# One 512-column product in place of two of 256, its streaming operand read in turns of 16 columns

## The chip, the cores and the metric

The kernel runs on one core of a Trainium2 chip. Its time is the device time of one execution in microseconds (us), as the median of several runs. TensorE multiplies 128x128 tiles of weights, which are loaded ahead of each product, with a streaming operand of up to 512 columns, and adds the results up in PSUM. VectorE, ScalarE and GpSimd do the elementwise work, and DMA queues bring the weights from HBM into SBUF.

## The reference

One layer of a hybrid encoder for 512 tokens of width 1024, in float32: two branches (a gated short convolution, and attention with a forget gate), their gated merge, a channel mixer with a hidden width of 2816, and three RMS norms.

```python
h = rms_norm(x, norm_mix_g[l])
proj = h @ w_in[l]
cb, cc, cin, q, k, v, f_logit, g_logit = jnp.split(proj, split_idx, axis=-1)
u = causal_dwconv(cc * cin, conv_mix_w[l])
y_conv = (cb * u) @ w_out_conv[l]
...
y_attn = o @ w_out_attn[l]
gates = jax.nn.sigmoid(g_logit + b_gate[l])
g_conv, g_attn = jnp.split(gates, 2, axis=-1)
x = x + (g_conv * y_conv + g_attn * y_attn) @ w_o[l]
h = rms_norm(x, norm_ffn_g[l])
up = causal_dwconv(h @ w_up[l], conv_ffn_w[l])
a, b = jnp.split(up, 2, axis=-1)
x = x + (jax.nn.silu(a) * b) @ w_down[l]
...
return rms_norm(x, norm_f_g)
```

## The kernel before

Activations lie transposed: 128 features on the partitions, the 512 tokens along the free dimension, one such block (`kb`) per 128 features. A product takes a 128x128 tile of weights as the stationary operand and streams tokens past it; a bank of PSUM holds 128 output features by 512 tokens, and the products over all input blocks add up in it.

Every float32 operand is split in two parts of the type float32r: a high part (a copy rounded by ScalarE, `wh`, `xgh`, `x1h`, `gh` ...) and a low part (the rest, by VectorE, `wl`, `xgl`, `x1l`, `gl` ...). `mm3` (line 166) multiplies three of the four combinations: high by high, low weights by high activations, high weights by low activations. It cuts the 512 tokens into two halves of 256 columns, so each call issues six products, each with its own load of weights: the two token halves with `wh` and `xh`, the two with `wl` and `xh`, the two with `wh` and `xl`. All products are kept in the order of the program.

Weights come in chunks of 128 rows by 1024 columns (512 KB) in one list, `stream`, whose order is that of use. `load` issues the DMAs three chunks ahead on the SyncE queue, `split` (line 138) makes the two parts one chunk ahead of TensorE (L151 on ScalarE, L152 on VectorE), into tiles `wh_...` and `wl_...` with two buffers each. The parts start at an offset within their tiles, `WOFF`: 0 elements for the high and 32 (128 bytes) for the low part. Pads (`PADL`, `PADR`) and this offset fix where operands lie. As the program is allocated, the activations that `mm3` streams start at a multiple of 512 bytes within a partition, the high weights 320 and the low weights 448 bytes past one; each tile of 128 columns is 512 bytes, so this holds for all of them.

The stages, with the names of their tiles: the v projection (`pa`, `pb`, L281 and L282, which stream the weights past the activations), q and k of the first two pairs of heads (`p_q`, `p_k`), attention (scores `s` at L410 and L411, transposes `tp` at L439, `attend` with `o` through `mm3` on 128 or 256 columns) with the remaining projections `p_in` put between its steps, then gates and the two branch outputs (`p_ga`, `p_gb`, `yc`, `ya`), the output projection `p_wo`, the mixer's up projection `p_up` (44 blocks of 128 features) and its down projection `pd` (8 blocks; the last is done in two token halves, `pdA` and `pdB`, so that the first half's norm and store can start early).

Of the kernel before, what the change touches and what calls it, by code (L numbers as in the profile page):

```python
# [9 lines left out]
F32R = mybir.dt.float32r  # L10
# [3 lines left out]
P = 128  # L14
# [12 lines left out]
NPP = 4  # L27
NCT = 5
BIG = 1e30
PADL, PADR = 48, 120  # L30


# [3 lines left out]
VW = 4 * HD + H  # L36
RC = 2 * (S + H)
WC = D + P
WOFF = {"h": 0, "l": 32}


@with_exitstack
def block_kernel(ctx, tc, xT, vecs, wv, win, wmix, wo, wup, wdn, outT):
# [3 lines left out]
    nc = tc.nc  # L47
# [3 lines left out]
    wp = ctx.enter_context(tc.tile_pool(name="wp", bufs=2))  # L51
    ps = ctx.enter_context(tc.tile_pool(name="ps", bufs=1, space=PSUM))

    def keep(ins):
        return tc.keep_in_program_order(ins)

    def bank(i, name):
        return ps.tile([P, S], F32, tag=f"b{i}", name=name)
# [14 lines left out]
    def col(i):  # L73
# [10 lines left out]
        out=strip[:, 3 * P :],  # L84
        in_=strip[:, 3 * P :],
        compare_op=ALU.is_ge,
        fill=BIG,
        base=0,
# [29 lines left out]
    for j in range(KB):  # L118
        for c in range(3):
            a, b = 8 * c * P, min(8 * c + 8, NP) * P  # L120
# [10 lines left out]
    def load(upto):  # L131
        for k in range(len(raws), min(upto, len(stream) - 1) + 1):
            nm, src, ncol = stream[k]
            raw = wp.tile([P, RC], F32, tag="raw", name=f"raw_{nm}", bufs=AHEAD + 1)[:, :ncol]
            keep((nc.scalar if k == 0 else nc.sync).dma_start(raw, src))
            raws.append(raw)

    def split(hl=None):

        k = len(parts)  # L140
        if k == len(stream):
            return
        nm, _, ncol = stream[k]
        load(k + AHEAD)
        hi, lo = hl or [
            wp.tile([P, WC], F32R, tag=f"w{x}", name=f"w{x}_{nm}", bufs=2)[:, WOFF[x] : WOFF[x] + ncol] for x in "hl"
        ]
        if k == 0:
            keep(nc.vector.tensor_copy(hi, raws[k]))
        else:  # L150
            order["hi"] = nc.scalar.activation(hi, raws[k], AF.Copy).ins  # L151
        order["lo"] = nc.vector.tensor_sub(lo, raws[k], hi.bitcast(F32)).ins  # L152
        parts.append((hi, lo))

    def chunk(name, hl=None):

        k = chunk.n
        chunk.n += 1
        assert stream[k][0] == name
        if len(parts) == k:  # L160
            split(hl)
        return parts[k]

    chunk.n = 0

    def mm3(out, wh, wl, xh, xl, start, stop):


        n = out.shape[-1]
        cut = [slice(a, a + 2 * P) for a in range(0, n, 2 * P)] if n > 2 * P else [slice(0, n)]  # L170
        trio = ((wh, xh), (wl, xh), (wh, xl))
        for i, (w, x) in enumerate(trio):
            for c, cs in enumerate(cut):
                keep(nc.tensor.matmul(  # L174
                    out[:, cs], w, x[:, cs],
                    start=start and i == 0 and c == 0,
                    stop=stop and i == 2 and c == len(cut) - 1,
                ))

    ex = cp.tile([P, NT], F32, tag="ex", name="ex")  # L180
    nc.gpsimd.memset(ex, -0.5)
# [44 lines left out]
    ap = at.enter_context(tc.tile_pool(name="ap", bufs=1, side="right"))  # L226
# [30 lines left out]
    for kb in range(KB):  # L257
        if kb + 2 < KB:
            load_x(kb + 2)
        wh, wl = chunk(f"v{kb}")  # L260
        x = xs[kb]
# [24 lines left out]
        trio = ((xgh, wh), (xgh, wl), (xgl, wh))  # L286
# [12 lines left out]
    def proj(idx, name, evac, bank):  # L299
        st = {}  # L300

        def half(i):
            if i == 0:
                st["w"] = chunk(f"in{idx}")
                st["p"] = bank(f"p_{name}")
            wh, wl = st["w"]
            for kb in range(4 * i, 4 * i + 4):
                ks = slice(kb * P, (kb + 1) * P)
                mm3(st["p"], wh[:, ks], wl[:, ks], xgh[:, kb, :], xgl[:, kb, :], kb == 0, kb == KB - 1)
            if i == 1:  # L310

                while len(parts) < chunk.n + 2:
                    split()
                with after_split():
                    evac(st["p"])

        return [lambda: half(0), lambda: half(1)]
# [127 lines left out]
    def attend(pr, half):  # L445
        o = bank(7, f"o{pr}{half}")
        nk = 2 * half + 2
        for e in range(2):
            th, tl = PT.pop((pr, e, half))
            for kb in range(nk):  # L450
                cs = slice(P, 2 * P) if kb == nk - 1 else slice(0, 2 * P)
                wh = vh[:, kb, pr, e : e + 2, :].rearrange("p a b -> p (a b)")
                wl = vl[:, kb, pr, e : e + 2, :].rearrange("p a b -> p (a b)")
                mm3(
                    o[:, cs], wh, wl, th[:, kb, cs], tl[:, kb, cs],
                    e == 0 and kb == 0, e == 1 and kb == nk - 1,
                )
        hs = slice(half * 2 * P, (half + 1) * 2 * P)
        nc.scalar.activation(oth[:, pr, hs], o[:, : 2 * P], AF.Copy)
        nc.vector.tensor_sub(otl[:, pr, hs], o[:, : 2 * P], oth.bitcast(F32)[:, pr, hs])  # L460


    def run_all(fs):
        for f in fs:
            f()

    split()
    split()

# [65 lines left out]
    for idx in late:  # L535
        kind, i = divmod(idx, 4)
# [7 lines left out]
    n = len(units)  # L544
    for i in range(n + LA):
        if i < n:
            scores(*units[i])
        take = 1 if i < n + LA - 1 else len(fill)
        for _ in range(min(take, len(fill))):
            fill.pop(0)()  # L550
        if 0 <= i - LT < n:
            transp(*units[i - LT])
        if 0 <= i - LA < n:
            pr, e, qb = units[i - LA]
            if e == 1 and qb % 2 == 1:
                attend(pr, qb // 2)
# [27 lines left out]
    for j in range(KB):  # L584
        gs = []
        if j == 0:
            evac_gate(0, gs)(gp[0])
            evac_gate(8, gs)(gp[1])
        else:
            run_all(proj(20 + j, f"ga{j}", evac_gate(j, gs), acc))  # L590
            run_all(proj(28 + j, f"gb{j}", evac_gate(8 + j, gs), acc))
        wh, wl = chunk(f"mix{j}")
        yc, ya = acc(f"yc{j}"), acc(f"ya{j}")
        for pp, hh, ll, o in ((yc, ych, ycl, 0), (ya, oth, otl, 4)):
            for k in range(4):
                ks = slice((o + k) * P, (o + k + 1) * P)
                mm3(pp, wh[:, ks], wl[:, ks], hh[:, k, :], ll[:, k, :], k == 0, k == 3)
        a, b = gs
        nc.vector.tensor_mul(a, a, yc)
        nc.vector.tensor_mul(b, b, ya)  # L600
        nc.gpsimd.tensor_add(a, a, b)
        nc.scalar.activation(mh[:, j, :], a, AF.Copy)
        nc.vector.tensor_sub(ml[:, j, :], a, mh.bitcast(F32)[:, j, :])
# [31 lines left out]
    def block(name, xh, xl):  # L635
        wh, wl = chunk(name)
        q = acc(f"p_{name}")
        for kb in range(KB):
            ks = slice(kb * P, (kb + 1) * P)
            mm3(q, wh[:, ks], wl[:, ks], xh[:, kb, :], xl[:, kb, :], kb == 0, kb == KB - 1)  # L640
        return q

    po = None
    for j in range(KB):
        if j == 0:
            po = lead(["wo0", "wo1"], mh, ml)
        p = po[j] if j < 2 else block(f"wo{j}", mh, ml)
# [13 lines left out]
    fp = ctx.enter_context(tc.tile_pool(name="fp", bufs=1))  # L661
# [6 lines left out]
    for j in range(NP):  # L668
# [12 lines left out]
        for s_ in range(2):  # L681
            p = pu[s_] if j == 0 else block(f"up{2 * j + s_}", x1h, x1l)
# [5 lines left out]
        a, b = uu  # L688
# [9 lines left out]
    def down(j, c, extra=False):  # L698
        k0 = 8 * c
        nk = min(8, NP - k0)  # L700
        hl = None
        if extra:
            hl = [
                fp.tile([P, WC], F32R, tag=f"wx{x}", name=f"wx{x}")[:, 80 + WOFF[x] :][:, : nk * P] for x in "hl"
            ]
        wh, wl = chunk(f"dn{j}{c}", hl)

        def f(p, ts, a=0, b=8):
            for k in range(a, min(b, nk)):
                ks = slice(k * P, (k + 1) * P)  # L710
                kb = k0 + k
                mm3(p, wh[:, ks], wl[:, ks], gh[:, kb, ts], gl[:, kb, ts], kb == 0, kb == NP - 1)

        return f

    full = slice(0, S)
    for j in range(KB - 1):
        p = bank(j % 4, f"pd{j}")
        for c in range(3):
            down(j, c)(p, full)  # L720
        nc.vector.tensor_add(x1[:, j, :], p, x1[:, j, :])
        square_into(ssq3, x1[:, j, :], j == 0, fp, f"sq3_{j}")
        nc.scalar.activation(x1[:, j, :], x1[:, j, :], AF.Copy, scale=col(GF + j))
# [16 lines left out]
    def fin_out(i, rc):  # L740
        hs = halves[i]
        pb = rstd_bc(rc, 2, i, f"n3{i}")[:, : S // 2]
        for g, (a, b) in enumerate(((0, 1), (1, 3), (3, 5), (5, 7), (7, 8))):
            y = x1[:, a:b, hs]
            nc.vector.tensor_mul(y, y, pb.unsqueeze(1).to_broadcast([P, b - a, S // 2]))
            keep((nc.sync, nc.scalar)[g % 2].dma_start(outT[:, a:b, hs], y))

    d0, d1, d2 = down(j, 0, True), down(j, 1), down(j, 2)
    for d in (d0, d1, d2):
        d(ph[0], halves[0])  # L750
# [91 lines left out]
```

## Time and profile before

| | us |
|---|---|
| median of 3 runs | 731.8 (730.42 to 734.79) |
| the profiled execution: its time | 734.09 |
| the profiled execution: its span, first to last instruction | 732.3 |
| VectorE busy in it | 400.5 |
| ScalarE busy in it | 292.7 |
| GpSimd busy in it | 140.6 |

The profile counts TensorE's products as PE and its loads of weights as PEld. Products are pipelined: the recorded time of one (the "mean ns") reaches from its start to its last result and overlaps the next, so the pace has to be read from the distance of starts, or from a stretch of time and the count of products in it. In a group's row, 128*128 is the size of the weights and 128x256 the streaming operand's partitions by columns.

### The profile page before, as it was taken

The numbers are of one execution on the slowest core, as the hardware profiler recorded it, in microseconds if no ns is written. First come the engines' busy times: TensorE is split into PE (matmuls) and PEld (weight loads), VectorE is DVE, ScalarE is ACT, GpSimd is POOL, SyncE is SP. The second block draws the span as 40 slices with busy tenths as digits, with TensorE's granted clock in tenths as the row PEclk, the third lists the DMA queues.
The fourth block names the chain that finished last, engine by engine and source line by source line (L and its number), as shares of the span: only waits on it lengthen the run. The fifth ranks groups of instructions, "written<-read, shape, count | busy, mean of one in ns | idle before, by whom it ended". The sixth has DMA issues, their size and how long they took to land.

```text
span 732.3 us, 14449 instructions
## 1 busy us (share of the span) xinstructions
PE 717.3 (98%) x6220; PEld 715.0 (98%) x6220; DVE 400.5 (55%) x582; ACT 292.7 (40%) x447; POOL 140.6 (19%) x158
## 2 busy tenths in 40 slices
PE   8989999999999999999999999999999999999995
PEld 7889999999999999999999999999999999999995
DVE  6477666765445445454456666666666673223323
ACT  6374545544433332333344344343353442222321
POOL 6515434322001000113311011101101100000100
PEclk9999999999999999999999999999999999999998
DMA  6523222221222332533313332332322423333303
GB/s 211 162 68 104 77 83 60 59 86 58 88 87 87 90 112 88 166 112 129 114 59 116 94 108 87 106 98 87 115 88 87 115 80 102 88 100 100 110 1 115
DMA packets 23296, 71.39 MB, mean 97 GB/s; under 512 B 2976, under 2 KB 5408, under 8 KB 23232
## 3 DMA queue, kind: packets, MB, share of 16 engines
q1 hardware_dynamic: 20848, 66.98, 29.7%
q0 software_dynamic: 1152, 2.17, 1.0%
q10 hardware_dynamic: 1232, 1.32, 0.6%
q8 instruction: 49, 0.80, 0.5%
q14 instruction: 15, 0.12, 0.1%
HBM read 68.29 MB, written 2.10 MB: 96 GB/s over the span
## 4 chain that ended last, share of the span: by engine, by line
PE 92%; DVE 2%; DMA 2%; ACT 1%; issue 1%; SPq 0%; POOLq 0%; POOL 0%; DVEq 0%; ACTq 0%
PE p_up L174 33%; PE pd L174 14%; PE p_in L174 14%; PE p_wo L174 6%; PE p_gb L174 5%; PE p_ga L174 5%; PE yc L174 3%; PE ya L174 3%; PE o L174 2%; DMA xs<-in_xT_dram 2%; PE tp L439 1%; PE pdA L174 1%; PE p_k L174 1%; PE s L410 1%; PE s L411 1%
## 5 line engine op out<-in xcount | busy, mean ns | idle before, releaser
L174 PE MATMUL p_up<-x1h,wh_up 128*128 128x256 f32 x704 | 137.3, 276 | 0.0
L174 PE MATMUL p_up<-x1l,wh_up 128*128 128x256 f32 x704 | 137.1, 276 | 0.0
L174 PE MATMUL p_up<-x1h,wl_up 128*128 128x256 f32 x704 | 137.0, 276 | 0.0
L174 PEld LDWEIGHTS p_up<-x1h,wh_up 128*128 128x128 f32 x704 | 106.1, 188 | 0.0
L174 PEld LDWEIGHTS p_up<-x1l,wh_up 128*128 128x128 f32 x704 | 106.0, 188 | 0.0
L174 PEld LDWEIGHTS p_up<-x1h,wl_up 128*128 128x128 f32 x704 | 105.9, 188 | 0.0
L690 POOL TENSOR_TENSOR fu<-fu,fu 128x512 f32<-128x512 f32 x22 | 28.4, 1293 | 211.2 <-DVE fu L368 198.3
L152 DVE TENSOR_TENSOR wl_in<-raw_in,wh_in 128x1024 fp32r<-128x1024 f32 x36 | 50.3, 1398 | 30.9 <-ACT wh_in L151 30.4
L152 DVE TENSOR_TENSOR wl_up<-raw_up,wh_up 128x1024 fp32r<-128x1024 f32 x44 | 53.7, 1220 | 14.5 <-ACT wh_up L151 14.5
L174 PE MATMUL pd<-gl,wh_dn 128*128 128x256 f32 x308 | 60.1, 276 | 0.0
L174 PE MATMUL pd<-gh,wh_dn 128*128 128x256 f32 x308 | 59.9, 276 | 0.0
L174 PE MATMUL pd<-gh,wl_dn 128*128 128x256 f32 x308 | 59.9, 276 | 0.0
L174 PE MATMUL p_in<-xgh,wh_in 128*128 128x256 f32 x288 | 56.8, 279 | 0.0
L174 PE MATMUL p_in<-xgl,wh_in 128*128 128x256 f32 x288 | 56.4, 277 | 0.0
L174 PE MATMUL p_in<-xgh,wl_in 128*128 128x256 f32 x288 | 56.4, 277 | 0.0
L152 DVE TENSOR_TENSOR wl_dn<-raw_dn,wh_dn 128x1024 fp32r<-128x1024 f32 (+1 forms) x23 | 26.0, 1132 | 54.9 <-ACT wh_dn L151 54.8
L151 ACT ACTIVATE wh_up<-raw_up 128x1024 fp32r<-128x1024 f32 x44 | 46.4, 1055 | 22.3 <-issue 13.4
L151 ACT ACTIVATE wh_in<-raw_in 128x1024 fp32r<-128x1024 f32 x36 | 38.2, 1061 | 42.5 <-PE ya L174 12.7
L151 ACT ACTIVATE wh_dn<-raw_dn 128x1024 fp32r<-128x1024 f32 (+1 forms) x23 | 22.7, 985 | 66.5 <-PE pd L174 66.2
L174 PEld LDWEIGHTS pd<-gl,wh_dn 128*128 128x128 f32 x308 | 46.5, 188 | 0.0
L174 PEld LDWEIGHTS pd<-gh,wh_dn 128*128 128x128 f32 x308 | 46.3, 188 | 0.0
L174 PEld LDWEIGHTS pd<-gh,wl_dn 128*128 128x128 f32 x308 | 46.3, 188 | 0.0
(223 smaller groups left out, 1611.7 us busy)
## 6 DMA issues: line engine op xcount, KB each, us to landing
raw_up<-in_wup_dram SPq DMA_DIRECT2D x44, 512.0 KB, 3.5
raw_in<-in_win_dram SPq DMA_DIRECT2D x36, 512.0 KB, 3.5
raw_dn<-in_wdn_dram SPq DMA_DIRECT2D x16, 512.0 KB, 3.5
raw_mix<-in_wmix_dram SPq DMA_DIRECT2D x8, 512.0 KB, 3.6
raw_wo<-in_wo_dram SPq DMA_DIRECT2D x8, 512.0 KB, 3.9
raw_dn<-in_wdn_dram SPq DMA_DIRECT2D x8, 384.0 KB, 3.3
xr<-in_xT_dram POOLq DMA_DIRECT2D x8, 256.0 KB, 3.8
raw_v<-in_wv_dram SPq DMA_DIRECT2D x7, 260.0 KB, 4.9
```

The source lines that it names most:

```text
L151: order["hi"] = nc.scalar.activation(hi, raws[k], AF.Copy).ins
L152: order["lo"] = nc.vector.tensor_sub(lo, raws[k], hi.bitcast(F32)).ins
L174: keep(nc.tensor.matmul(out[:, cs], w, x[:, cs], start=start and i == 0 and c == 0, stop=stop and i == 2 and c == len(cut) - 1,))
L410: keep(nc.tensor.matmul(s[:, :nn], QT[pr][:, e, qs], KA[pr][:, e, :nn], start=True, stop=False))
L411: keep(nc.tensor.matmul(s[:, :nn], QB[pr % 2][: KR[e], e, qs], KBt[pr % 2][: KR[e], e, :nn], start=False, stop=True))
L439: keep(nc.tensor.transpose(tp[:, ks], pt[:, ks], ident))
L690: nc.gpsimd.tensor_mul(a, a, b)
```

## The change

`mm3` issues three products of 512 columns where it issued six of 256. The streaming operand and the output are read and written through a pattern of three steps: with `h=2`, `c=16`, the 512 columns count as two halves of 16 groups of 16 columns, and the groups of the two halves follow each other in turn (columns 0 to 15, 256 to 271, 16 to 31, 272 to 287 ...). The output is written in the same turns, so each result lands where it did. `attend`, whose operands have 128 or 256 columns, passes `plain=True` and reads in order. The last down block, which calls `mm3` with 256 columns, takes turns between two runs of 128.

Both parts of the weights start 16 elements (64 bytes) into their tiles. As the program is allocated, every weight tile that `mm3` uses then lies 384 bytes past its streaming operand, modulo 512.

```diff
+GC = 16
...
-WOFF = {"h": 0, "l": 32}
+WOFF = 16
...
-            wp.tile([P, WC], F32R, tag=f"w{x}", name=f"w{x}_{nm}", bufs=2)[:, WOFF[x] : WOFF[x] + ncol] for x in "hl"
+            wp.tile([P, WC], F32R, tag=f"w{x}", name=f"w{x}_{nm}", bufs=2)[:, WOFF : WOFF + ncol] for x in "hl"
...
-    def mm3(out, wh, wl, xh, xl, start, stop):
-
-
-        n = out.shape[-1]
-        cut = [slice(a, a + 2 * P) for a in range(0, n, 2 * P)] if n > 2 * P else [slice(0, n)]
-        trio = ((wh, xh), (wl, xh), (wh, xl))
-        for i, (w, x) in enumerate(trio):
-            for c, cs in enumerate(cut):
-                keep(nc.tensor.matmul(
-                    out[:, cs], w, x[:, cs],
-                    start=start and i == 0 and c == 0,
-                    stop=stop and i == 2 and c == len(cut) - 1,
-                ))
+    def turns(ap):
+
+        return ap.rearrange("p (h i c) -> p i h c", h=2, c=GC)
+
+    def mm3(out, wh, wl, xh, xl, start, stop, plain=False):
+
+        f = (lambda ap: ap) if plain else turns
+        keep(nc.tensor.matmul(f(out), wh, f(xh), start=start, stop=False))
+        keep(nc.tensor.matmul(f(out), wl, f(xh), start=False, stop=False))
+        keep(nc.tensor.matmul(f(out), wh, f(xl), start=False, stop=stop))
...
-                    e == 0 and kb == 0, e == 1 and kb == nk - 1,
+                    e == 0 and kb == 0, e == 1 and kb == nk - 1, plain=True,
...
-                fp.tile([P, WC], F32R, tag=f"wx{x}", name=f"wx{x}")[:, 80 + WOFF[x] :][:, : nk * P] for x in "hl"
+                fp.tile([P, WC], F32R, tag=f"wx{x}", name=f"wx{x}")[:, 80 + WOFF :][:, : nk * P] for x in "hl"
```

## The prediction

> **What bounds the kernel now.** I read the page first (share of each engine, chain of waits), then a table of the engines' busy time by stage, then the groups of TensorE products by shape, then single instructions in the timeline.
>
> ```profile
> span 732.3 us, 14449 instructions
> PE 717.3 (98%) x6220; PEld 715.0 (98%) x6220; DVE 400.5 (55%) x582; ACT 292.7 (40%) x447; POOL 140.6 (19%) x158
> PE 92%; DVE 2%; DMA 2%; ACT 1%; issue 1%; SPq 0%; POOLq 0%; POOL 0%; DVEq 0%; ACTq 0%
> ```
>
> TensorE is the path: 92% of the chain. PE has exactly as many weight loads (PEld) as products, and both are busy 98%, so it is still open which of the two sets the pace. The stages (start and end, then busy time and instructions of each engine, granted clock, DMA):
>
> ```profile
> core 0: us, PE busy (x) PEld busy (x) DVE busy (x) ACT busy (x) POOL busy (x), PEclk, DMA share, GB/s
> 0.00:62.00 62.00, 54.75 (x417) 53.50 (x418) 40.20 (x60) 34.77 (x61) 30.46 (x46) 0.94 0.47 143
> 62.00:194.00 132.00, 132.00 (x1130) 131.32 (x1129) 85.20 (x193) 62.33 (x139) 41.66 (x59) 1.00 0.24 75
> 194.00:360.00 166.00, 166.00 (x1466) 166.00 (x1465) 78.45 (x85) 58.02 (x70) 25.54 (x22) 1.00 0.35 108
> 360.00:602.00 242.00, 242.00 (x2137) 242.00 (x2136) 156.97 (x198) 103.46 (x135) 30.00 (x23) 1.00 0.32 96
> 602.00:706.00 104.00, 104.00 (x920) 104.00 (x920) 31.74 (x32) 30.14 (x36) 10.07 (x6) 1.00 0.30 89
> ```
>
> From 194 to 706 us one product starts every 113 ns (242.00 us / 2137 = 113.2; 166.00 / 1466 = 113.2; 104.00 / 920 = 113.0). What sets 113 ns? An attention product of 128 columns stands beside others of 256:
>
> ```profile
> 122.57 0.22 PE L174 MATMUL o<-pth,vh 128*128 128x128 f32 x1
> 122.63 0.28 PE L174 MATMUL o<-pth,vl 128*128 128x128 f32 x1
> 122.74 0.27 PE L174 MATMUL o<-ptl,vh 128*128 128x128 f32 x1
> 122.85 0.33 PE L174 MATMUL o<-pth,vh 128*128 128x256 f32 x1
> ```
>
> The first occupies TensorE for 0.06 us (122.57 to 122.63), but the next two, with as few columns, take 0.11 us each: the time of a 256-column product. Half the columns and the same pitch means that the load of the next weights is what is waited for, one per 0.11 us. So the paired 256-column products of today run at the pace of their loads, and each weight tile is loaded twice, once for each token half.
>
> **The change: what it removes.** `mm3` issues one 512-column product for each pair, so half the loads go. The pairs follow from the loops, and these groups confirm them (each tile has three such rows):
>
> ```profile
> L174 PE MATMUL p_up<-x1h,wh_up 128*128 128x256 f32 x704 | 137.3, 276 | 0.0
> L174 PE MATMUL pd<-gh,wh_dn 128*128 128x256 f32 x308 | 59.9, 276 | 0.0
> L174 PE MATMUL p_in<-xgh,wh_in 128*128 128x256 f32 x288 | 56.8, 279 | 0.0
> L174 PE MATMUL p_wo<-mh,wh_wo 128*128 128x256 f32 x128 | 25.0, 276 | 0.0
> L174 PE MATMUL p_ga<-xgh,wh_in 128*128 128x256 f32 x112 | 21.8, 276 | 0.0
> L174 PE MATMUL yc<-ych,wh_mix 128*128 128x256 f32 x64 | 12.5, 277 | 0.0
> ```
>
> Pairs: p_up 704 x 3 / 2 = 1056, pd 462, p_wo 192, p_ga and p_gb 168 each, yc and ya 96 each: 2238 steady pairs at 2 x 113.25 = 226.5 ns. p_in has 432 pairs that run a little slower, since scores and transposes break the rhythm:
>
> ```profile
> 96.50 2.76 PE p_in L174 x24
> ```
>
> 2.76 us / 12 pairs = 230 ns. p_q and p_k (48 pairs each) lie before 62 us, in the stage that waits for splits and in part runs at half clock.
>
> **What it adds: a 512-column product, whose load is hidden.** With 0.11 us per load and over 0.21 us per product the load no longer sets the pace; the columns do. The trace has plain 512-column products only among the scores:
>
> ```profile
> 177.47 0.39 PE L411 MATMUL s<-kb,qb 128*128 128x512 f32 x1
> 177.47 0.42 PEld L174 LDWEIGHTS p_in<-xgh,wh_in 128*128 128x128 f32 x2
> 177.70 0.40 PE L174 MATMUL p_in<-xgh,wh_in 128*128 128x256 f32 x2
> ```
>
> and, as groups by shape (us busy, mean ns of one):
>
> ```profile
> L174 PE MATMUL o<-pth,vh 128*128 128x128 f32 x16 | 3.5, 220 | 0.0
> L411 PE MATMUL s<-kb,qb 128*128 128x512 f32 x4 | 1.6, 392 | 0.0
> L411 PE MATMUL s<-kb,qb 68*128 68x512 f32 x4 | 1.6, 397 | 0.0
> L411 PE MATMUL s<-kb,qb 128*128 128x384 f32 x4 | 1.3, 337 | 0.0
> ```
>
> Upper end: the L411 product has its weights in place and still holds TensorE from 177.47 to 177.70, 230 ns, more than a pair of today's (226.5). Its recorded 392 ns thus holds some 162 ns that overlap the next product; the other L411 form, 397, gives 235. The next load starts in the same instant (177.47), so it reads SBUF while the product streams.
>
> Lower end: the rate of the columns alone. At half clock the columns, not the loads, set the pace:
>
> ```profile
> 56.13 0.63 PE L174 MATMUL p_k<-xgl,wh_in 128*128 128x256 f32 x2
> 56.55 0.63 PE L174 MATMUL p_k<-xgh,wh_in 128*128 128x256 f32 x2
> 56.98 0.63 PE L174 MATMUL p_k<-xgh,wl_in 128*128 128x256 f32 x2
> ```
>
> ```profile
> 56.00:57.00 1.00, 1.00 (x7) 1.00 (x7) 0.30 (x2) 0.86 (x2) 0.84 (x3) 0.50 0.81 70
> ```
>
> Four products take 0.85 us (56.13 to 56.98) at clock 0.50: 0.83 ns a column, 0.415 at full clock, so 512 columns need 213 ns and no layout gets below that.
>
> Value taken: the 128-column product that did not wait is the cleanest row: 220 ns recorded, less 162 to 163 of overlap, 57 to 58 ns, which is also its 0.06 us in the timeline. With 384 more columns at 0.415 (159 ns) this is **217 ns**. It assumes that a product's extra over its columns is paid once (4 ns), so that the further 13 ns of L411 are stalls between its reading and the load's, and that the change removes them. The reason to believe this lies in the addresses, not in a row: turned, the product walks 512 bytes (modulo 512) in 256 columns, some 107 ns, and a load reads its 512 bytes in about the same time. Both run at one pace, 384 bytes apart, where plain reading would overtake the load once. That fails if the load reads from the other end; no row shows its direction.
>
> The Trainium skill disagrees on the cause: its page "TensorE: Matmul & The Clock Gate", section "Step-by-step: what each phase is for", says that weights have a read port of their own and take nothing from the streaming operand, and "Back-to-back issue gap" gives N / 2.4 + 2.5 ns, an estimate of 215.8 ns for 512 columns in any layout. The 230 ns above are against it for plain reading; by it, the gain would be an estimated 30 us and the turns would be idle.
>
> **Moved and left alone.** The offset of the split weights (320 and 448 bytes before, 384 for both now, modulo 512) also moves the stream of the v products (L281, L282, 384 of them). These range from 118 to 122 ns now; going to 113 or rising as much is 384 x 7 ns = under 3 us in a stage that partly waits for splits: taken as 0. The last output block (132 half-width products) stays at the pace of its loads; at most its 15 jumps of address each show, 15 x 0.415 x 132 = 0.8 us; taken as 0. Attention's `attend` keeps plain reading. A few split and evacuation steps on VectorE and ScalarE change order within attention; these engines have slack there (85 and 62 of 132 us). DMA, splits and evacuations keep their counts, and what covers them shrinks to 24 x 217 = 5.2 us per chunk:
>
> ```profile
> L152 DVE TENSOR_TENSOR wl_up<-raw_up,wh_up 128x1024 fp32r<-128x1024 f32 x44 | 53.7, 1220 | 14.5 <-ACT wh_up L151 14.5
> L151 ACT ACTIVATE wh_up<-raw_up 128x1024 fp32r<-128x1024 f32 x44 | 46.4, 1055 | 22.3 <-issue 13.4
> raw_up<-in_wup_dram SPq DMA_DIRECT2D x44, 512.0 KB, 3.5
> ```
>
> 1.06 us + 1.22 us of split and a landing of 3.5 us, asked for three chunks ahead, still fit. VectorE, next in line, goes from 157 of 242 us to 157 of 231 in p_up. If the split became late, TensorE would wait at a chunk's start; nothing near that shows.
>
> **The sum.** Steady: 2238 x (226.5 - 217) = 21.3 us. p_in: 432 x (230 - 217) = 5.6 us. p_q and p_k: 0.3 us (the few that wait for nothing). Together 27.2 us, so a span of 705.1 from 732.3. The profiled execution took 734.1, 2.3 above the median of the runs (731.8); against that median, **705 us** (731.8 - 27.2 = 704.6). Of its own unknowns: 213 ns gives 731.8 - 37.6 = 694, 220 ns 714.
>
> **The rivals.**
> Columns that cost more (C). From L411, 384 to 512 columns, 392 - 337 = 55 ns per 128, not 53. Then 57 + 3 x 55 = 222 ns, saving 2238 x 4.5 + 432 x 8 = 13.5 us: 718 us. For it: the two shapes follow each other in the same code. Against: a conflict with the load is in both, and it is what the change aims at.
>
> The turns do not avoid the stall (B), the change not doing what it says: the price is that of L411, 230 to 235 ns. 2238 x 3.5 = 7.8 us more (p_in unchanged), 740 us; at 235 ns 2238 x 8.5 + 432 x 5 = 21 us, 753. For it: weights read from the other end would still cross the stream.
>
> The jumps cost (A), the other side. Each product leaps 31 times between halves, in what it reads and in what it writes to PSUM; no product of this profile has a broken pattern, so a jump's price is bounded below by 0 and above, as an estimate, by two column times of the half-clock row. It decides from (226.5 - 217) / 31 = 0.31 ns, three quarters of a column. At one column (0.415 ns) a product is 230 ns and the time 739; at two, 243 ns, 2238 x 16.5 + 432 x 13 = 42.5 us more: 774. Against it: each run is 16 columns long, 64 bytes. The Trainium skill speaks for it: "PSUM — Partial Sum Buffer", section "Specifications (TRN2)", says that any non-contiguous pattern slows matmuls significantly. No run here shows it yet.
>
> The gain is lost to another engine or eaten half by A or B (225 to 229 ns): 728 to 736.
>
> **How the numbers follow.** Forecast (214 to 220 ns, 697 to 714 us) 0.62; C 0.13; A 0.13; B 0.07; the last, about no change, 0.05. Half a percent (3.7 us) is what a measurement of this kernel can tell. Faster 0.62 + 0.13 = 0.75, same 0.05, slower 0.13 + 0.07 = 0.20. The range goes from 696 (1 us for the v products) over C and the case of no change to the mild ends of A and B, 740; the likeliest case alone is 697 to 714.
>
> **What would show it.** Right: PE and PEld near 3450 instructions; p_up groups of x352 with 128x512; starts 217 ns apart; PE still over 97% busy but PEld far below, since loads fall to about half the time; p_up's stage 230 to 232 us instead of 242. A or B: same counts, starts 230 ns or more apart (B near L411's 230 to 235, A anywhere above, and alike in all stages). C: 222 ns. Another engine: idle PE before chunks, released by DVE wl or ACT wh. I am wrong if the pitch is 226 or more, or if the pitch falls and the span does not.

## The result, and the profile after

The changed kernel takes 767.88 us (median of 4 runs, 767.46 to 768.49), beside 732.64 us for the kernel before in the same measurement: a ratio of 1.0482, 95% interval 1.0447 to 1.0516. It is 4.8% slower, where 705 us and 3.7% faster were forecast, and outside the range of 696 to 740.

From the page of the profile after, the span, the engines' shares, the chain by engine, and the group of one p_up product:

```profile
span 765.8 us, 8917 instructions
PE 751.9 (98%) x3454; PEld 609.3 (80%) x3454; DVE 400.9 (52%) x582; ACT 293.4 (38%) x447; POOL 140.5 (18%) x158
PE 93%; DMA 2%; DVE 2%; ACT 1%; issue 1%; POOL 0%; SPq 0%; POOLq 0%; DVEq 0%; ACTq 0%
L174 PE MATMUL p_up<-x1h,wh_up 128*128 128x512 f32 x352 | 142.0, 403 | 0.0
```

The change did what it says: 6220 - 2766 = 3454 products and as many loads, and the loads now rest a fifth of the time (80% busy). TensorE is still 93% of the chain and never waits in p_up (idle 0.0). So nothing else became the bound: each product of 512 columns itself takes longer. The timeline shows by how much:

```profile
420.20 0.40 PE L175 MATMUL p_up<-x1h,wl_up 128*128 128x512 f32 x1
420.44 0.40 PE L176 MATMUL p_up<-x1l,wh_up 128*128 128x512 f32 x1
420.68 0.40 PE L174 MATMUL p_up<-x1h,wh_up 128*128 128x512 f32 x1
```

One start every 0.24 us: 240 ns, where a pair took 226.5 and the forecast had 217. The recorded 403 ns less 240 leave 163 ns of overlap with the next product, the amount that the prediction found (162 to 163), so at full clock, and where nothing is waited for, recorded times can again be turned into distances of starts. The stages after (start and end, busy time and instructions of each engine, clock, DMA), cut where p_in, the gates, p_up and pd begin and end:

```profile
0.00:61.00 61.00, 54.94 (x327) 48.12 (x328) 39.85 (x59) 34.47 (x61) 29.96 (x46) 1.00 0.44 145
61.00:197.00 136.00, 136.00 (x694) 112.63 (x693) 85.70 (x194) 63.67 (x140) 42.22 (x59) 1.00 0.22 73
197.00:373.00 176.00, 176.00 (x747) 139.91 (x746) 78.51 (x85) 57.92 (x70) 25.53 (x22) 1.00 0.31 102
373.00:628.00 255.00, 255.00 (x1072) 202.24 (x1072) 156.96 (x197) 103.06 (x134) 29.87 (x23) 1.00 0.28 91
628.00:739.00 111.00, 111.00 (x464) 87.86 (x463) 31.94 (x32) 30.31 (x36) 10.12 (x6) 1.00 0.28 82
```

Every stage that `mm3` fills grew alike: p_up from 242 to 255 us, pd from 104 to 111, the gates and output projections from 166 to 176. By the prediction's own sum, 2238 x (240 - 226.5) = 30.2 us and 432 x some 10.5 = 4.5 us for p_in, together 34.7; the span grew by 33.5. The first stage gave about 1.7 us back: p_in begins at 61 instead of 62.6 us, and the stage ran at clock 1.00 instead of 0.94.

### The profile page after: what moved, and what is told of

Its sections match the earlier page's. It is cut to its first block, busy times and chain, and to the rows that moved or that the text cites. A ratio compares the mean times of both kernels' runs of the same rounds, so it can differ in the third digit from the quotient of the medians.

```text
span 765.8 us, 8917 instructions
## 1 busy us (share of the span) xinstructions
PE 751.9 (98%) x3454; PEld 609.3 (80%) x3454; DVE 400.9 (52%) x582; ACT 293.4 (38%) x447; POOL 140.5 (18%) x158
## 4 chain that ended last, share of the span: by engine, by line
PE 93%; DMA 2%; DVE 2%; ACT 1%; issue 1%; POOL 0%; SPq 0%; POOLq 0%; DVEq 0%; ACTq 0%
PE p_up L174 11%; PE p_up L176 11%; PE p_up L175 11%; PE pd L176 5%; PE pd L175 5%; PE pd L174 5%; PE p_in L174 5%; PE p_in L176 5%; PE p_in L175 5%; PE p_wo L176 2%; PE p_wo L175 2%; PE p_wo L174 2%; PE p_gb L176 2%; PE p_gb L175 2%; PE p_gb L174 2%; PE p_ga L176 2%
## 5 line engine op out<-in xcount | busy, mean ns | idle before, releaser
L174 PE MATMUL p_up<-x1h,wh_up 128*128 128x512 f32 x352 | 142.0, 403 | 0.0
L175 PE MATMUL p_up<-x1h,wl_up 128*128 128x512 f32 x352 | 141.9, 403 | 0.0
L176 PE MATMUL p_up<-x1l,wh_up 128*128 128x512 f32 x352 | 141.9, 403 | 0.0
L174 PEld LDWEIGHTS p_up<-x1h,wh_up 128*128 128x128 f32 x352 | 66.9, 190 | 17.5
L174 PE MATMUL pd<-gh,wh_dn 128*128 128x512 f32 x154 | 62.1, 403 | 0.0
L175 PE MATMUL pd<-gh,wl_dn 128*128 128x512 f32 x154 | 62.1, 403 | 0.0
L176 PE MATMUL pd<-gl,wh_dn 128*128 128x512 f32 x154 | 62.1, 403 | 0.0
L174 PE MATMUL p_in<-xgh,wh_in 128*128 128x512 f32 x144 | 58.3, 405 | 0.0
L176 PE MATMUL p_in<-xgl,wh_in 128*128 128x512 f32 x144 | 58.0, 403 | 0.0
L175 PE MATMUL p_in<-xgh,wl_in 128*128 128x512 f32 x144 | 58.0, 403 | 0.0
L682 DVE TENSOR_TENSOR fz<-p_up,rb_n 128x512 f32<-128x512 f32 x44 | 30.2, 688 | 35.0 <-PE p_up L176 34.8
```

Source lines behind the costliest of these rows:

```text
L174: keep(nc.tensor.matmul(f(out), wh, f(xh), start=start, stop=False))
L175: keep(nc.tensor.matmul(f(out), wl, f(xh), start=False, stop=False))
L176: keep(nc.tensor.matmul(f(out), wh, f(xl), start=False, stop=stop))
L682: nc.vector.tensor_mul(z, p, rb2)
```

## The experiments

What had to be told apart: whether the leaps of the address cost the time (theory J), the streaming operand meeting the load of the next weights in SBUF (theory S), or the columns themselves (theories C and F); whether reading or writing pays; and what part the offset of the weights has. (These letters, and the B and P that join them below, name theories of the experiments, not the rivals of the prediction.) Several experiments make the blocks of p_up in different ways within one kernel, so that their distances of starts can be read from one profile; their names end in letters that stand for the offset or the size.

**Turns taken out.** The 512-column products are read and written in order, with everything else as after the change.

```diff
-        f = (lambda ap: ap) if plain else turns
+        f = lambda ap: ap
```

> The change without the turns: 512-column products read and written in order, weights 384 bytes past. Theory J (each leap between halves costs one column time, 0.415 ns, 31 per product; the profile after shows 240 ns per product): 240 - 13 = 227 ns per product, so 2670 x 13 = 35 us less than after, about 733, equal to before. Theory S (the stalls come from the weight load meeting the stream, and turning makes that worse or better): plain reading overtakes the load once, as in L411, 230 ns or more, 740 us or above. Theory C (a column costs more than 0.415 ns whatever the order): 240 ns as after, 768 us.

Measured: 747.64 us (before in the same measurement 733.16; ratio 1.0209, 1.0164 to 1.0255). The turns cost 767.9 - 747.6 = 20.2 us; the other 14.5 us of the loss are there without them. The group of p_up in this kernel:

```profile
L175 PE MATMUL p_up<-x1h,wl_up 128*128 128x512 f32 x352 | 138.9, 395 | 0.0
```

395 - 163 = 232 ns, between what J (227) and the change (240) would have. J has the direction, but the size is the one that S gave (230 ns or more, 740 us or above).

**The offset alone.** The kernel before, 256-column products, with the weights' offset of the change.

```diff
-WOFF = {"h": 0, "l": 32}
+WOFF = {"h": 16, "l": 16}
```

> The kernel before with only the offset of the weights changed: both parts 384 bytes past, products still 256 columns each. If the pace of 113 ns is that of the weight load alone (my prediction) or the offset does not matter: 113 ns and 732 us. If the offsets of 320 and 448 avoid stalls that 384 brings (theory S): 116 to 120 ns a product as pdA and pdB show after the change (120), up to 5532 x 6.7 = 37 us more, 769.

Measured: 760.52 us (ratio 1.038, 1.0339 to 1.0422), nearly as slow as the change.

```profile
L174 PE MATMUL p_up<-x1h,wl_up 128*128 128x256 f32 x704 | 140.9, 281 | 0.0
```

281 instead of 276 ns each, 5 x 5532 = 28 us. The stream and the load of the weights do get in each other's way: 64 bytes of offset are worth 27 us, and a pace set by the loads alone, whatever the stream does, would not have moved.

**Offsets by order of reading.** In the blocks of p_up:

```diff
+        how, c, m = mode or (("p" if plain else "t"), GC, P)
+        rd = turned(c) if how in "tr" else same
+        wr = turned(c) if how in "tw" else same
...
+        v = PLAN.get(int(nm[2:])) if nm[:2] == "up" else None
+        wo_ = 16 * v[2] if v else WOFF
```

> The change with the blocks of p_up made in 24 ways, one after the other: plain 512, turned 512, and split 256, each at eight offsets of the weights (a to h: 320, 384, 448, 0, 64, 128, 192, 256 bytes past the stream modulo 512). Read is the distance of starts in each. Theory J: turned 240 ns and plain 227 at every offset, split 113 everywhere. Theory S: each of the three moves by 5 to 15 ns with the offset, and turned at some offset falls to 217 to 227.

The chain of waits of this kernel gives the time of each block's 24 products (48 when split); its columns are start, length, what:

```profile
386.51 5.59 PE p_plain_a L187 x24
403.18 5.45 PE p_plain_d L187 x24
430.77 5.76 PE p_turn_a L187 x24
448.05 5.76 PE p_turn_d L187 x24
476.85 5.46 PE p_split_a L187 x48
488.00 5.65 PE p_split_c L187 x48
493.65 5.75 PE p_split_d L187 x48
```

Divide by 24. Read in order, a product takes 227 ns at offsets of 0 and 256 bytes (d, h) and up to 233 at the others (a is 320). Split, it is the reverse: 5.46 / 48 = 114 ns at 320, 120 at 0. The offset of one load by itself does not tell the pace, though: with both parts at 448 (c) a split product takes 118 ns, while the kernel before, with the high parts at 320 and the low ones at 448, keeps 113. Turned, it is 240 at each of the eight offsets. So under turns the offset no longer matters; but the price is more than the worst offset costs plain reading. Theory S alone falls, since nothing brings turned reading below 240.

**Groups and sides.** At the change's offset, three blocks of each form (72 products, 144 when split): groups of 8, 16, 32, 64 and 128 columns (gd to gh), read or write alone, and weights of 64 columns (narrow).

```diff
+        rd = turned(c) if how in "tr" else same
+        wr = turned(c) if how in "tw" else same
...
+                mw = P if (start and i == 0) or (stop and i == 2) else m
+                keep(nc.tensor.matmul(
+                    wr(out[:mw, cs]), w[:, :mw], rd(x[:, cs]),
```

> The change with the blocks of p_up made in 14 ways at the offset of 384: groups of 8, 16, 32, 64 and 128 columns, plain, turns in the read alone or in the write alone (these leave tokens in another order), and, in three ways, weights of 64 columns in all but the first and last products of a block, which leaves out half of those blocks' features. Theory J: 227 ns plus 0.415 ns per leap: groups of 8: 253, 16: 240, 32: 233, 64: 230, 128: 228; which of read and write pays shows in the one-sided ways (240 for one, 227 for the other; at groups of 8, 253). Theory S: no steady order with the number of leaps, and the write alone costs nothing. Weights of 64 columns halve the load: if the split pace of 113 ns is the load's, it falls to 109 or below; if it is the columns' own, it stays 113.

Again from the chain of waits:

```profile
386.69 16.80 PE p_plain L185 x72
403.49 17.52 PE p_gd L185 x72
421.00 17.28 PE p_ge L185 x72
455.33 16.73 PE p_gg L185 x72
488.79 17.28 PE p_rdonly L185 x72
506.07 16.80 PE p_wronly L185 x72
540.38 16.74 PE p_wreight L185 x72
557.13 16.56 PE p_narrow_plain L185 x72
573.69 16.82 PE p_narrow_split L185 x144
590.51 17.28 PE p_narrow_turn L185 x72
607.78 17.29 PE p_splitw L185 x144
```

Turns in the write alone cost nothing (16.80, as plain, and 16.74 for groups of 8, wreight); turns in the read alone cost all (17.28, as both). By size, 17.52 / 72 = 243 ns for groups of 8, 240 for 16, 237 for 32, 232 for 64 and for 128, beside 233 read in order at this offset. Fewer leaps are cheaper, but not at one price each: 32 more leaps from groups of 16 to 8 add 3 ns, not 13. Half the load (narrow) leaves a turned product at 240 ns: the load is not what delays it. At this offset a split product falls from 120 to 117 ns with half the load, and one of 512 columns in order from 233 to 230, so there the load has a part.

**Distance of the two runs.** Perhaps a leap pays because both runs lie at the same place modulo 512 bytes. This is theory B. The read's distance was varied, from 256 (letter a) over 240 (c) and 224 (e) to 128 columns (q). Two lines of the plan of blocks, by number of the block: name, start of the weights in elements, columns streamed, columns of weights, and the steps of the read.

```diff
+    4: ('sta_c', 0, 512, 128, (0, [16, 16], [240, 2], [1, 16])),
+    5: ('sta_e', 0, 512, 128, (0, [16, 16], [224, 2], [1, 16])),
```

> The change with the blocks of p_up read in turns of 16 columns, but with other distances between the two runs than 256 columns: 256, 248, 240, 224, 192, 160 and 128 (then columns are read twice and others not at all, and the output is written in order, so these blocks' values are not the layer's), each with the weights 320, 384 and 512 bytes past. Theory B (the read pays at a leap because both runs lie at the same place modulo 256 or 512 bytes): 240 ns at distances of 256 and 192 or 128 columns (1024, 768, 512 bytes), and 217 to 227 at 224 or 240 (896, 960 bytes). Theory J (any leap pays): 240 at every distance. Theory S (the load in the way): a change with the offset of the weights, none seen so far for turns.

```profile
386.87 5.76 PE p_sta_a L237 x24
404.24 5.84 PE p_sta_e L237 x24
```

240 to 243 ns at all seven distances and three offsets. Theory B falls: it is the leap, not where it lands. (As built, these blocks write their output in turns of 16, not in order as expected; by the experiment before, that costs nothing.)

**Width of the load, length of the stream.** Weights of 128, 64 and 32 columns against streams of 512 to 128, read in order.

```diff
+    4: ('full_dy', 48, 256, 128, None),
...
+    7: ('half_dy', 48, 256, 64, None),
...
+    10: ('quarter_dy', 48, 256, 32, None),
```

> The change with the blocks of p_up read in order, with weights of 128, 64 and 32 columns (in all but the first and last products of a block; the other features of these blocks are left out) and streams of 512, 384, 256 and 128 columns (the other tokens left out), at weights 512 and 384 bytes past. Theory F (the stream itself loses one cycle in 16 or 17 columns): 227 ns for 512 columns at any width of weights, 170 for 384, 113 for 256. Theory S (the loss is the load's, which lasts as long as its columns): with weights of 32 columns 512 take 217 to 219 ns, 384 take 164, 256 take 110, and full weights add the same 8 to 15 ns to each.

These quick blocks overtake the splits in places, so the groups' mean times are used. First 256-column products with full, half and quarter weights at offset 0, then their loads, then 128-column products with half weights (shortest, median and longest time):

```profile
L237 PE MATMUL p_full_dy<-x1l,wh_up 128*128 128x256 f32 x14 | 4.0, 283 | 0.0
L237 PE MATMUL p_half_dy<-x1h,wl_up 128*64 128x256 f32 x16 | 4.4, 277 | 0.0
L237 PE MATMUL p_quarter_dy<-x1h,wl_up 128*32 128x256 f32 x16 | 4.4, 277 | 0.0
L237 PEld LDWEIGHTS p_full_dy<-x1h,wh_up 128*128 128x128 f32 x16 | 3.1, 191 | 0.0
L237 PEld LDWEIGHTS p_half_dy<-x1h,wh_up 128*64 128x64 f32 x14 | 1.9, 134 | 0.0
L237 PE MATMUL p_half_dz<-x1h,wl_up x16: 222/223/308, 475.3 to 576.3; 128*64 128x128 f32 x16
```

These are the rows that answer the forecast. At this offset the full load costs a 256-column product some 6 ns (283 - 163 = 120). With half or a quarter of the load it still records 277 ns, the 113 to 114 ns of the kernel before (276), although the load is shorter by 57 ns (191 to 134). If the load set that pace, these would have fallen to 109 or below. The columns have that pace of their own: 113.3 / 256 = 0.443 ns each. A product of 128 columns, by contrast, does follow the load. With full weights the waiting `o` products of the kernel before record 276 ns, with half weights it is 223 here, so 113 and 60 ns:

```profile
L174 PE MATMUL o<-pth,vl 128*128 128x128 f32 x16 | 4.4, 276 | 0.0
```

No width of weights gave theory S its 217 to 219 ns for 512 columns: in order, at offset 0, the `x1l` products record 391 ns with full weights and 394 with a quarter, 228 and 231 ns. For 384 columns it is 170 to 176 ns at the two offsets, where F had 170 and S 164.

**Steps of 8 bytes, and backwards.** Plain reading at 23 offsets, most of them in steps of 8 bytes, and with the last column first.

```diff
+    11: ('fine_j', 50, 512, 128, None),
...
+    28: ('rev_d', 48, 512, 128, (511, [-1, 512])),
```

> The change with the blocks of p_up read in order, 512 columns, weights at 17 offsets in steps of 8 bytes from 448 to 576 bytes past (fine a to q) and six from 208 to 288 in steps of 16 (far), and read backwards, last column first, at eight offsets in steps of 64 from 320 (rev; tokens of these blocks come out in reverse). Theory S: the pitch moves smoothly with the offset between 227 and 236, lowest where load and stream never meet in one stretch, perhaps under 225; backwards it changes with the direction in which the load reads: lower than in order (217 to 225) if the load reads its columns last first, higher (240) if first to last. Theory F: 227 is the floor, forwards and backwards.

```profile
472.51 5.61 PE p_fine_q L237 x24
494.73 5.44 PE p_far_d L237 x24
528.01 5.60 PE p_rev_d L237 x24
```

Forwards the steps lie between 5.44 / 24 = 227 and 234 ns, in no smooth course, where S had a smooth one; none goes below. Backwards it is 233 ns at each of the eight offsets, again independent of them. Three orders of reading, three prices: 227 at best in order, 233 backwards, 240 in turns.

**Hardly any load.** Weights of 1, 16 and 64 columns at eight offsets, read in order (edit as above, other widths).

> The change with the blocks of p_up read in order, 512 columns, with weights of 1, 16 and 64 columns (in all but the first and last products of a block; the other features of these blocks are left out), each at eight offsets (a to h: 320, 384, 448, 0, 64, 128, 192, 256 bytes past). Theory F + load (the stream alone takes 227 ns, 17 cycles for 16 columns, and the load's reading adds 0 to 8 ns by its offset): with weights of one column 227 ns at every offset, with 64 columns 227 to 232. Theory S (the load is the whole loss over 213 ns): with one column 214 to 218 ns. Theory P (the offset acts on the stream by itself): the same spread of 227 to 235 at any width.

```profile
387.57 5.56 PE p_one_a L237 x24
426.47 5.49 PE p_one_h L237 x24
```

With one column of weights the products take 229 to 232 ns at all offsets. All three theories miss in part: the loss over 213 ns does not go with the load (against S, by which the load is the whole of it), the offset loses half its effect with it (against P, by which the offset acts on the stream by itself; 3 ns of spread, where full loads showed 6), and yet the tiny load does not reach the 227 of a full one at a good offset (against F, by which 227 is the stream's own time). A good offset seems to put load and stream in step; that is inferred, not shown.

**At half clock.** Four quick blocks let TensorE wait until its clock drops, then come a turned, a plain and a reversed one.

```diff
+    5: ('fast', 48, 128, 32, None),
+    6: ('turn', 48, 512, 128, (0, [16, 16], [256, 2], [1, 16])),
+    7: ('plain', 48, 512, 128, None),
+    8: ('rev', 48, 512, 128, (511, [-1, 512])),
```

> The change with the blocks of p_up in groups of seven: four quick ones (128 columns with weights of 32, the rest left out), so that TensorE waits for splits and its clock may drop, then one turned, one plain and one read backwards, 512 columns each at weights 512 bytes past. At half clock: if the losses are cycles of TensorE itself, turned takes 480 ns (576 cycles), plain 454 (544) and backwards 467 (560). If they come from a supply of columns that has a pace of its own, all three take 427 ns (512 cycles).

The timeline of one turned block, before and after its clock came back, and the stretch that gives the clock of its first part (0.50):

```profile
443.30 0.63 PE L237 MATMUL p_turn<-x1l,wh_up 128*128 128x512 f32 x1
443.73 0.63 PE L237 MATMUL p_turn<-x1h,wh_up 128*128 128x512 f32 x1
444.15 0.63 PE L237 MATMUL p_turn<-x1h,wl_up 128*128 128x512 f32 x1
...
446.06 0.40 PE L237 MATMUL p_turn<-x1h,wh_up 128*128 128x512 f32 x1
446.30 0.40 PE L237 MATMUL p_turn<-x1h,wl_up 128*128 128x512 f32 x1
```

```profile
443.00:445.00 2.00, 2.00 (x6) 1.53 (x5) 0.04 (x1) 0.70 (x2) 1.27 (x1) 0.50 0.57 219
```

At half clock a turned product takes (444.15 - 443.30) / 2 = 425 ns, twice 213: the turns cost nothing there. At full clock the same block takes 240. So the loss is not a fixed number of TensorE's cycles, which would have made it 480. What fits is that the columns are supplied at a pace of their own, which depends on the order of reading and shows only where TensorE is faster. That is inferred; where in the chip this pace arises, no run shows. No plain or reversed block fell into half clock here, but plain 512-column products did in the `p_k` of the plain kernel under the next heading, at clock 0.50:

```profile
56.09 0.63 PE L174 MATMUL p_k<-xgh,wh_in 128*128 128x512 f32 x1
56.51 0.63 PE L175 MATMUL p_k<-xgh,wl_in 128*128 128x512 f32 x1
56.94 0.63 PE L176 MATMUL p_k<-xgl,wh_in 128*128 128x512 f32 x1
```

```profile
56.10:58.60 2.50, 2.50 (x7) 1.99 (x6) 2.44 (x3) 1.43 (x2) 2.44 (x4) 0.50 0.47 182
```

(56.94 - 56.09) / 2 = 425 ns, as turned; at full clock the same kernel takes 226 to 227 ns. Plain reading too loses only at full clock.

**The best offset, whole kernels.** Both the plain and the turned version with the weights 512 bytes past.

```diff
-WOFF = 16
+WOFF = 48
```

> The change without the turns and with the weights 512 bytes past (0 modulo 512), the best offset of the plain blocks so far (227 ns): 2670 x (240 - 227) = 35 us less than after, 733, the same as before within 1 per cent. If the last offset of another stage or the other engines matter: 735 to 745.

Plain: 733.03 us, before 732.11, ratio 1.0007 (0.9989 to 1.0025): no difference.

```profile
L175 PE MATMUL p_up<-x1h,wl_up 128*128 128x512 f32 x352 | 137.0, 389 | 0.0
```

389 - 163 = 226 ns: a 512-column product at its best equals a pair of the kernel before, with half the loads.

> The change as it is, with the weights 512 instead of 384 bytes past. If turns make the offset idle, as the blocks of the third experiment say: 240 ns per product and 768 us. If 384 had been needed for them: 770 to 790; if 512 is better for them as for plain reading: 750 to 760.

Turned: 767.35 us (ratio 1.0476, 1.0433 to 1.0519), the same as the change at 384. Under turns the offset is idle in the whole kernel too.

No version beat the kernel before; its pairs already run at the columns' best pace found (113.3 ns for 256).

## Why the prediction was wrong

- **TensorE bounds the kernel, and its pace decides:** right. The counts, the share of TensorE, the slack of the other engines and the sum by 2238 and 432 pairs held (34.7 us by 240 ns, 33.5 measured).
- **The loads set the pace of 113 ns:** this step failed. The row behind it was read rightly as far as it goes: a 128-column product does wait for the next load, 0.11 us. But from it I took that the 256-column products wait for loads alone. Two limits nearly coincide there: a load takes about 0.11 us, and 256 columns take 113 ns. With weights of 64 or 32 columns the 256 still take 113 to 114, while 128 columns with weights of 64 fall to 60.
- **217 ns for 512 columns:** failed for the same reason. It added 384 columns at 0.415 ns, from the half-clock row, as if a column took half as long at full clock. Measured, a column in order costs 227 / 512 = 0.443 ns at full clock. The term of the sum was thus 2238 x (226.5 - 227), about nothing, before any harm by the turns: halving the loads had nothing to gain (733.0 us at the best offset, beside 732.1). Rival C had come near this (222 ns) and was given 0.13, on the ground that its extra was the conflict that the change removes.
- **The 13 ns of L411 are stalls that the turns remove:** half right. Offset-dependent stalls exist (227 to 234 ns in order), and the turns remove the dependence. But they replace it by 240 at every offset. The reason given, a load and a turned stream that keep 384 bytes apart, is not borne out: with 0 between them it is the same 240.
- **Rival A, the jumps cost:** the one that came true, at 0.13; the forecast had put this cost at nothing. Its 31 leaps at one column time, 13 ns, is what groups of 16 cost over the best plain product (240 - 227), but that match is luck: as a price per leap it is wrong (groups of 8 add 3 ns, not 13), and its base of 217 put it at 739 us. It also left open which side pays: the read does, the write does not. "PSUM — Partial Sum Buffer", section "Specifications (TRN2)", of the Trainium skill says that any non-contiguous pattern slows matmuls significantly; the write in runs of 16 columns shows no cost here (16.80 us for 72 products, as plain).
- **Rival B, the turns do not avoid the stall:** not what happened. It had the 230 to 235 ns of L411; turned products take 240 at any offset and with half the load, so what they pay is not that stall left in place.
- **The separate ports:** the Trainium skill, "TensorE: Matmul & The Clock Gate", section "Step-by-step: what each phase is for", says that loading the next weights takes no read bandwidth from the running product. The kernel before at the other offset (760.5 us) speaks against taking the two as free of each other here, and so do the 120 and 114 ns of 256 columns with a full and a half load at one offset. The estimate of 215.8 ns for 512 columns, from the formula that the Trainium skill gives on that page, section "Back-to-back issue gap", for a single product by itself, is not reached by any steady form of these runs at full clock; 227 is the best.
- **Offset moved at no cost elsewhere:** small but not nothing; the last block's products went from 113 to 120 ns (132 x 7 = 0.9 us), about as bounded. It is the offset and not the jumps: read in order at 384 they take as long (282 ns recorded, as after the change).
- **Slips that did not move the forecast:** by its own sum 220 ns give 713 us, not 714, and 225 to 229 ns give 726 to 737, not 728 to 736. The v products are 192 (six groups of 32), not 384.

The loss splits so: some 14.5 us come with 512-column products at an offset of 384 bytes, all of which goes when the offset is 512 (733.0 us), and 20.2 us come with the turns. The split depends on the offset: at 512 the turns cost all of it, 767.35 - 733.03 = 34.3 us.

## What to carry to other kernels

When a product's pace equals that of its load, do not conclude that the load sets it: narrow the load and see if the pace moves, before a change is built on it. A rate taken at half clock need not double at full clock: here 512 columns went from 425 ns to 227 or 240, not to 213. Read a float32r stream in order and fit the offset of the weights to it by measurement; an order that makes the offset idle can still cost more than the worst offset (240 ns here, beside 234).

## What the runs showed of the hardware

- A float32r stream in order takes at best 227 ns for 512 columns at full clock (some 547 column times of 0.415 ns, half of the 425 / 512 = 0.83 ns at half clock, so about 17 for 16 columns), and 113 to 114 for 256, the latter with weights of 128, 64 or 32 columns at a good offset; at half clock there is no such loss (425 ns for 512). Why stays open.
- The order of reading sets the pace: 227 to 234 ns in order by the offset of the weights, 233 backwards and 240 in turns of 16 columns, these two at any of eight offsets.
- 64 bytes of offset between weights and stream moved a whole kernel of 256-column products by 3.8%.
- PSUM written in turned runs of 8 or 16 columns costs nothing over writing in order (16.74 and 16.80 us for 72 products, beside 16.80).
